# The PLE gate of a hybrid MLA/GLA layer on one core: its first 512 columns as one block of 512 in place of two of 256

## The chip, the cores and the metric

The kernel runs on one core of a Trainium2 chip. The metric is device microseconds of one execution; the figure of a kernel is the median of its runs. A trace of one profiled execution stands beside it: for each engine (PE for the matrix engine, DVE for vectors, ACT for activations, POOL, and SP, which issues the DMAs) when each instruction ran and what it waited for.

## What is computed

One layer, 1024 tokens, model width 1024, all in fp32: an input projection, latent attention (MLA, 8 heads, 64 columns without and 32 with rotary position) and a gated linear attention (GLA) side by side, a sigmoid-gated merge, an output projection, and at the end a gate of per-layer embeddings:

```
merged = sigmoid(merge_a) * y_a + sigmoid(merge_b) * y_b
x = x + merged @ w_out[l]

e = rmsnorm(p[l] @ w_ple[l], ple_norm_g[l])
g_ple = jax.nn.sigmoid(rmsnorm(x, ple_gate_norm_g[l]) @ w_ple_gate[l])
x = x + g_ple * e
return rmsnorm(x, final_norm_g)
```

The change is in the second last product, `rmsnorm(x) @ w_ple_gate`, which is 1024 x 1024 by 1024 x 1024.

## The kernel before

**Precision and matmuls.** Each fp32 operand is kept as a high part (fp32r) and a low rest. `split` makes them: ACT copies the high part (L127), DVE subtracts (L128). A product is three matmuls (`mm3`, L145 to L147): high by high, high by low, low by high. A weight tile is loaded by SP (`load_w`, L137) and split.

**Buffers.** Nearly everything takes its memory from numbered slots of 128 x 1024 fp32 (512 KB): `alloc` takes the slot that has been free the longest, `drop` gives it back. There are NSLOT = 35, and NMORE = 4 more are opened when the GLA part is over.

**Order of work.** The program is written as generators that are advanced in turn, but the order on each engine is not the written one: a scheduler places all instructions by a timeline of its own when the program is built, for all engines at once, and waits between engines are set after that. So each engine and SP run a fixed list.

**Attention** (about 500 to 760 us). Heads go in pairs. `make_pair` projects q and then k of both heads in one product, in two halves of 512 tokens, and splits the result into the odd head's buffers (qh, ql, kh, kl). The even head's 64 rows are then copied to its own buffers by DMA (L864: qh<-qh, ql<-ql, kh<-kh, kl<-kl), and after such a copy has landed the odd head's rotary rows are written over the place they came from (L871 for q, L867 for k). `scores` and `weighted` follow for each head and each half: scores s (L145 to L147), row maximum (L914), exp (L924), transposes of p into pt (L963) and their split, products o with vp (L954, L955), and og (L976 to L978) with a gate gt that was loaded (L945) and scaled with the row sums that came through DRAM (L943, L946). Units of work of several heads and of other parts (the q/k projection of the next pair from w_qk and w_qr, and `embed`, which computes e from in_pT and in_w_ple and scales it by in_ple_g, gb) lie between them. The y projection (from oh, ol, the split of og) begins before the last head is done and adds to ta (L992, L993), which is split into mh, ml.

**Gate** (881 us on). `stream` multiplies by w_out, and x2 and its normed, transposed parts gh, gl come out (L1126, L1127). `load_pg` loads gate weights: w_pgA for the first 512 columns, in two halves of 256 with two tiles each (each tile holds 4 of the 8 row blocks), w_pgB for the last 512 with four tiles. For each of the two halves and each of the 8 token blocks `block` makes 24 matmuls of 256 columns, a tanh (L1183), two DVE products (L1184, L1186) and a square with a row sum (L1188). Then come the last 512 columns, where each token block's row sum is finished, its scale is found (`newton1`) and it is written out (L1216 to L1221); the last token block is cut in two of 256 columns.

Of the kernel before, what the change touches and what calls it, by code (L numbers as in the profile page):

```python
# [16 lines left out]
P = 128  # L17
S = 1024
D = 1024
HALF = 512  # L20
# [1 line left out]
HEADS = 8  # L22
SCALE = (64 + 32) ** -0.5
NSLOT = 35
NMORE = 4
NTMP = 6
NG = 6

# [24 lines left out]
def hybrid_kernel(tc, a, out):  # L53
    nc = tc.nc
    from contextlib import ExitStack

    with ExitStack() as ctx:
# [12 lines left out]
        def uid(name):  # L70
            count[0] += 1
            return f"{name}_{count[0]}"
# [7 lines left out]
        def drop(*ts):  # L80
            for t in ts:
                if id(t) in held:
                    i, _ = held.pop(id(t))
                    free.append(i)
# [4 lines left out]
        def t2(name, dt=F32):  # L89
            return tp.tile([P, HALF], dt, tag="t2", name=uid(name))  # L90
# [44 lines left out]
        def load_w(src, w, eng=None):  # L135
            raw = alloc(F32, "wr")
            nc.sync.dma_start(raw[:, :w], src)  # L137
            hi = alloc(F32R, "wh")
            lo = hi[:, HALF:S] if w <= HALF else alloc(F32R, "wl")
            split(hi[:, :w], lo[:, :w], raw[:, :w], eng)  # L140
            drop(raw)
            return hi, lo
# [103 lines left out]
        d_e = [dr.tile([P, S], F32, name=f"d_e{m}") for m in range(8)]  # L246
# [25 lines left out]
        with tc.tile_pool(name="ps0", bufs=1, space=PSUM) as ps0:  # L272
# [162 lines left out]
            for tb in range(8):  # L435
                ps = get("d", "gv")
                for kt in range(8):
                    hi, lo = wv[kt // 2]
                    c = slice((kt % 2) * HALF, (kt % 2 + 1) * HALF)
# [11 lines left out]
        with tc.tile_pool(name="psG", bufs=1, space=PSUM) as psG:  # L451
# [293 lines left out]
            pools[1] = ctx.enter_context(tc.tile_pool(name="slots2", bufs=1))  # L745
            free.extend(range(NSLOT, NSLOT + NMORE))

# [52 lines left out]
        with tc.tile_pool(name="psB", bufs=1, space=PSUM) as psB:  # L800
# [75 lines left out]
            for tb in range(8):  # L876
                ps = get("d", "v")
                hi, lo = wv_
                for kt in range(2):
                    c = slice(kt * HALF, (kt + 1) * HALF)  # L880
# [176 lines left out]
            for n in range(16):  # L1057
# [6 lines left out]
                per = 2 if hf == 0 else 1  # L1064
# [42 lines left out]
        with tc.tile_pool(name="psC", bufs=1, space=PSUM) as psC:  # L1107
            get = psum_pool({"d": (HALF, 5), "t": (HALF, 3)}, psC)
            getC.append(get)
            for n, _ in enumerate(ya):  # L1110
                if n == 11 - n_pre:
                    w_first = load_w(a["w_out"][0:P, :], S)
            drop(*ooh, *ool)


            gh, gl = [], []
            x2 = big(F32, "x2")
            x2m = x2.rearrange("p (t c) -> p t c", t=8)

            def ev_x2(m):  # L1120
                def ev(h, ps):
                    if h == 0:
                        gh.append(alloc(F32R, "gh"))
                        gl.append(alloc(F32R, "gl"))
                    xs = t2("xr")
                    nc.sync.dma_start(xs, a["xT"][m * P : (m + 1) * P, hs(h)])  # L1126
                    nc.vector.scalar_tensor_tensor(xs, ps, 0.5, xs, op0=ALU.mult, op1=ALU.add)  # L1127
                    split_gain(gh[m][:, hs(h)], gl[m][:, hs(h)], xs, col(V_PG + m))
                    late.append((m, h, xs))

                return ev

            def turn():
                m, h, xs = late.pop(0)
                pt = get("t", "xt")
                for j in range(4):
                    nc.tensor.transpose(pt[:, j * P : (j + 1) * P], xs[:, j * P : (j + 1) * P], ident)
                nc.scalar.activation(x2m[:, 4 * h : 4 * h + 4, m * P : (m + 1) * P], pt.rearrange("p (t c) -> p t c", t=4), AF.Copy)

            late = []  # L1140

            def load_pg(b):
                src, n = (a["w_pgA"][b * P : (b + 1) * P], 2) if b < 2 else (a["w_pgB"], 4)
                return [load_w(src[:, j * S : (j + 1) * S], S) for j in range(n)]

            wpg = [None] * 3
            jobs = [(a["w_out"][m * P : (m + 1) * P, :], P, 8, ev_x2(m)) for m in range(8)]
            for n, _ in enumerate(stream(get, jobs, mh, ml, w_first)):
                if n == 15:
                    wpg[0] = load_pg(0)  # L1150
                if n > 1:
                    turn()
            turn()
            drop(*mh, *ml)

            fg = alloc(F32, "fg")
            nc.sync.dma_start(fg, a["fin_g"].to_broadcast([P, S]))
            r2 = []
            dn = cp.tile([P, 1], F32, name="dn")
            nc.gpsimd.memset(dn, D * EPS)  # L1160
            for tb in range(8):
                s1, r = small("x2s", 1), small("x2r", 1, bufs=8)
                sq = alloc(F32, "sq")
                nc.scalar.activation(sq, x2m[:, tb, :], AF.Square, accum_out=s1)
                drop(sq)
                newton1(r, s1, dn, D)
                nc.vector.tensor_scalar(r, r, 0.5, None, op0=ALU.mult)
                r2.append(r)
            s3 = cp.tile([P, 32], F32, name="s3")
            QW = 256  # L1170

            def block(tb, b, c0, w, et):

                bw, per = (QW, 4) if b < 2 else (HALF, 2)
                o = b * QW + c0
                ps = get("d", "pg")
                for kt in range(8):
                    hi, lo = wpg[b][kt // per]
                    c = slice((kt % per) * bw + c0, (kt % per) * bw + c0 + w)
                    xs = slice(tb * P, (tb + 1) * P)  # L1180
                    mm3(ps[:, :w], gh[kt][:, xs], gl[kt][:, xs], hi[:, c], lo[:, c], kt == 0, kt == 7)
                g_ = t2("g")[:, :w]
                nc.scalar.activation(g_, ps[:, :w], AF.Tanh, scale=r2[tb])  # L1183
                nc.vector.scalar_tensor_tensor(et, g_, 1.0, et, op0=ALU.add, op1=ALU.mult)  # L1184
                xq = x2m[:, tb, o : o + w]
                nc.vector.scalar_tensor_tensor(xq, et, re_[:, tb : tb + 1], xq, op0=ALU.mult, op1=ALU.add)  # L1186
                k = tb * 4 + b + (c0 > 0)
                nc.scalar.activation(g_, xq, AF.Square, accum_out=s3[:, k : k + 1])  # L1188

            for b in range(2):  # L1190
                wpg[b + 1] = load_pg(b + 1)
                for tb in range(8):
                    et = t2("et")[:, :QW]
                    nc.sync.dma_start(et, d_e[tb][:, b * QW : (b + 1) * QW])
                    block(tb, b, 0, QW, et)
                for w_ in wpg[b]:
                    drop(*w_)
            ets = []
            for tb in range(8):
                ets.append(alloc(F32, "et"))  # L1200
                nc.sync.dma_start(ets[tb][:, :HALF], d_e[tb][:, HALF:S])
            for tb in range(8):

                cut = HALF if tb < 7 else 256
                k0, n = tb * 4, 2 + (tb == 7)
                if tb == 7:
                    block(tb, 2, 0, cut, ets[tb][:, 0:cut])
                s1, r = small("fs", 1), small("fr", 1)
                nc.vector.tensor_reduce(s1, s3[:, k0 : k0 + n], axis=mybir.AxisListType.X, op=ALU.add)
                nc.vector.tensor_scalar(s1, s1, D * EPS, None, op0=ALU.add)  # L1210
                c0 = cut % HALF
                block(tb, 2, c0, HALF - c0, ets[tb][:, c0:HALF])
                newton1(r, s3[:, k0 + n : k0 + n + 1], s1, D)
                for h in range(2):
                    xo = x2m[:, tb, hs(h)]
                    nc.gpsimd.tensor_tensor(xo, xo, fg[:, hs(h)], op=ALU.mult)  # L1216
                    if h:
                        nc.scalar.activation(xo, xo, AF.Copy, scale=r)
                    else:
                        nc.vector.tensor_scalar(xo, xo, r, None, op0=ALU.mult)  # L1220
                    nc.sync.dma_start(out[tb * P : (tb + 1) * P, hs(h)], xo)  # L1221
# [3 lines left out]
def _tiles(w, cols, width=P):  # L1225

    K = w.shape[0]
    n = len(cols) // width
    w = w[:, np.asarray(cols)].reshape(K // P, P, n, width)
    return np.ascontiguousarray(w.transpose(2, 1, 0, 3).reshape(n * P, K // P * width))  # L1230
# [26 lines left out]
def _layout(inputs):  # L1257
    g = {k: np.asarray(v) for k, v in inputs.items()}
    o = {}
# [3 lines left out]
    w = g["w_in"][0]  # L1263
# [9 lines left out]
    for pr in range(4):  # L1273
        A, B = 2 * pr, 2 * pr + 1
        n = np.concatenate([np.arange(h * 96, h * 96 + 64) for h in (A, B)])
# [7 lines left out]
    full = np.arange(D)  # L1283
# [1 line left out]
    o["w_gla_br"] = _tiles(g["w_gla_br"][0], full)  # L1285
    o["w_out"] = _tiles(g["w_out"][0], full)
    o["w_ple"] = np.ascontiguousarray(g["w_ple"][0])
    o["w_pgA"] = _tiles(g["w_ple_gate"][0], full[:512], 256)
    o["w_pgB"] = _tiles(g["w_ple_gate"][0], full[512:], 512)
    o["ple_g"] = np.ascontiguousarray(g["ple_norm_g"]).reshape(1, D)  # L1290
    o["fin_g"] = np.ascontiguousarray(g["final_norm_g"]).reshape(1, D)
    o["w_gk_up"] = np.ascontiguousarray(np.tile(g["w_gk_up"][0], (4, 1)))
# [22 lines left out]
```

## Time and profile before

| | us |
|---|---|
| median of 3 runs (lowest, highest) | 984.31 (984.19, 984.76) |
| the profiled execution | 983.49 |
| its span in the trace | 981.7 |
| PE busy in it | 955.8 |
| granted clock of PE, mean | 0.99 |
| first matmul of the gate at | 881.2 |

The span runs from the first instruction to the last; 1.8 us of the execution lie around it. The profiled execution is 0.8 us under the median. A row of a list of instructions gives start, duration, engine, line, operation, output <- inputs, and in square brackets the idle time in front with the one that ended it. Matmuls overlap in the records, so their pace is read from start to start.

### The profile page before, as it was taken

The page shows a single profiled execution, that of the slowest core. Times are in us where ns is not written, and L with a number is a line of the kernel's source. Part 1 is how long each engine was busy: PE and PEld are TensorE (multiplying, and loading weights), DVE is VectorE, ACT ScalarE, POOL GpSimd, SP SyncE. Part 2 cuts the span into 40 slices and gives each one's busy share as a digit, 9 for nine tenths or more (in the row PEclk, how much of TensorE's full clock was granted, in tenths as well). Part 3 has the DMA queues.
Part 4 walks back from the last instruction along what each step waited for, and adds up shares of the span by engine and source line. Part 5 has one row for each costly group of instructions (what it writes and reads, how often), then busy time and mean ns, then how long its engine had stood idle before and what let it go on. Part 6 is the DMA issues. An engine that isn't in the chain of part 4 may idle for free.

```text
span 981.7 us, 14101 instructions
## 1 busy us (share of the span) xinstructions
PE 955.8 (97%) x5216; PEld 794.3 (81%) x5216; DVE 590.2 (60%) x1227; ACT 413.1 (42%) x800; POOL 128.1 (13%) x103
## 2 busy tenths in 40 slices
PE   7999999999999999999999999997999999999995
PEld 5887877887887887888888778886888788889985
DVE  6737765574474474433476469785757863239666
ACT  7306731331331342321333257676885432228333
POOL 2100000000000000001101012235363000000422
PEclk9999999999999999999999999997999999999998
DMA  7200211122222122211253844537146761136112
GB/s 281 94 22 22 65 43 43 57 84 86 76 108 86 63 79 86 97 65 43 82 181 127 230 121 121 133 98 177 49 147 229 254 208 65 49 119 188 53 69 103
DMA packets 47828, 105.70 MB, mean 108 GB/s; under 512 B 6736, under 2 KB 9616, under 8 KB 47760
## 3 DMA queue, kind: packets, MB, share of 16 engines
q1 hardware_dynamic: 47760, 104.81, 33.1%
q8 instruction: 41, 0.67, 0.3%
q14 instruction: 27, 0.22, 0.1%
HBM read 72.18 MB, written 25.20 MB: 99 GB/s over the span
## 4 chain that ended last, share of the span: by engine, by line
PE 86%; DVE 6%; ACT 3%; DMA 3%; issue 2%; SPq 0%; DVEq 0%; ACTq 0%
PE d L145 19%; PE d L147 18%; PE d L146 18%; PE pt L963 3%; PE pg L147 3%; PE pg L146 3%; PE pg L145 3%; PE L L559 2%; PE o L955 2%; PE s L146 2%; PE o L954 2%; PE s L147 2%; PE s L145 2%; PE o L690 1%; DMA kl<-kl 1%
## 5 line engine op out<-in xcount | busy, mean ns | idle before, releaser
L145 PE MATMUL d<-xh,wh 128*128 128x512 f32 x544 | 215.9, 400 | 2.8 <-ACT xh L132 2.6
L146 PE MATMUL d<-xl,wh 128*128 128x512 f32 x544 | 214.5, 395 | 0.1
L147 PE MATMUL d<-xh,wl 128*128 128x512 f32 x544 | 213.3, 393 | 0.1
L145 PEld LDWEIGHTS d<-xh,wh 128*128 128x128 f32 x544 | 103.0, 190 | 28.1 <-ACT xh L132 4.6
L127 ACT ACTIVATE wh<-wr 128x1024 fp32r<-128x1024 f32 (+4 forms) x81 | 76.2, 943 | 114.3 <-DMA wr<-in_w_in 40.4
L146 PEld LDWEIGHTS d<-xl,wh 128*128 128x128 f32 x544 | 103.0, 189 | 21.9 <-DVE xl L133 0.8
L147 PEld LDWEIGHTS d<-xh,wl 128*128 128x128 f32 x544 | 102.7, 189 | 21.9 <-DVE wl L128 0.5
L128 DVE TENSOR_TENSOR wl<-wr,wh 128x1024 fp32r<-128x1024 f32 (+2 forms) x59 | 74.6, 1267 | 71.2 <-ACT wh L127 71.1
L145 PE MATMUL pg<-wh,gh 128*128 128x256 f32 (+1 forms) x200 | 62.7, 314 | 0.0
L146 PE MATMUL pg<-wl,gh 128*128 128x256 f32 (+1 forms) x200 | 62.5, 313 | 0.0
L147 PE MATMUL pg<-wh,gl 128*128 128x256 f32 (+1 forms) x200 | 62.5, 313 | 0.0
L128 DVE TENSOR_TENSOR pt<-pt,pt 128x512 fp32r<-128x512 f32 (+1 forms) x96 | 51.4, 550 | 17.1 <-ACT pt L127 16.9
L494 ACT ACTIVATE z<-z 128x512 f32<-128x512 f32 x32 | 20.2, 631 | 98.0 <-DVE z L466 94.2
L924 ACT ACTIVATE p<-p,nm 128x128 f32<-128x128 f32 (+3 forms) x64 | 49.3, 772 | 21.2 <-DVE nm L914 21.1
L466 DVE TENSOR_TENSOR z<-d,rb 128x512 f32<-128x512 f32 x32 | 22.1, 690 | 51.3 <-PE d L147 51.3
L127 ACT ACTIVATE pt<-pt 128x512 fp32r<-128x512 f32 (+1 forms) x96 | 44.6, 485 | 15.5 <-PE pt L963 13.6
L145 PE MATMUL d<-mh,wh 128*128 128x512 f32 x128 | 50.7, 399 | 0.0
L146 PE MATMUL d<-ol,wh 128*128 128x512 f32 x128 | 50.1, 392 | 0.4 <-DVE ol L128 0.4
L147 PE MATMUL d<-mh,wl 128*128 128x512 f32 x128 | 50.2, 392 | 0.0
L147 PE MATMUL d<-oh,wh 128*128 128x512 f32 x128 | 50.1, 391 | 0.0
L146 PE MATMUL d<-ml,wh 128*128 128x512 f32 x128 | 49.9, 390 | 0.0
L145 PE MATMUL d<-oh,wh 128*128 128x512 f32 x128 | 49.9, 395 | 0.0
(263 smaller groups left out, 1924.4 us busy)
## 6 DMA issues: line engine op xcount, KB each, us to landing
wr<-in_w_in SPq DMA_DIRECT2D x33, 512.0 KB
d_ta<-z SPq DMA_DIRECT2D x16, 256.0 KB
d_tb<-z SPq DMA_DIRECT2D x16, 256.0 KB
tb<-d_tb SPq DMA_DIRECT2D x16, 256.0 KB
d_zb<-tb SPq DMA_DIRECT2D x16, 256.0 KB
d_e<-er SPq DMA_DIRECT2D x16, 256.0 KB
ta<-d_ta SPq DMA_DIRECT2D x16, 256.0 KB
zb<-d_zb SPq DMA_DIRECT2D x16, 256.0 KB
```

The source lines that it names most:

```text
L127: nc.scalar.activation(dst_hi, src, AF.Copy)
L128: (eng or nc.vector).tensor_tensor(dst_lo, src, f(dst_hi), op=ALU.subtract)
L145: nc.tensor.matmul(ps, lh, rh, start=first, stop=False)
L146: nc.tensor.matmul(ps, lh, rl, start=False, stop=False)
L147: nc.tensor.matmul(ps, ll, rh, start=False, stop=last)
L466: nc.vector.tensor_tensor(z, ps, rb[:, hs(h)], op=ALU.mult)
L494: nc.scalar.activation(z, z, AF.Tanh, scale=0.5)
L559: nc.tensor.matmul(L[:, hd * HALF + c * P : hd * HALF + (c + 1) * P], lt[rows(hd), cs], rt[rows(hd), cs], start=True, stop=True,)
L924: nc.scalar.activation(pt[:, :w], pt[:, :w], AF.Exp, bias=nm, scale=-1.0, accum_out=den)
L954: nc.tensor.matmul(po[:, n0:], vv, ts_[:, n0:HALF], start=kb == 0, stop=False)
L955: nc.tensor.matmul(po[:, n0:], vv, ts_[:, HALF + n0 : S], start=False, stop=kb == nk - 1)
L963: nc.tensor.transpose(pt[:, j * P : (j + 1) * P], pq[j][:, kb * P : (kb + 1) * P], ident)
```

## The change

NMORE becomes 8, and the scratch that the program sets aside for DMAs with dynamic addresses becomes 1024 bytes, which makes room for the four slots. The gate's weight becomes one array w_pg of two halves of 512 columns, four tiles each; the first half is one pass over the token blocks with blocks of 512, as the second was. The row sums have one column fewer per token block.

```diff
-NMORE = 4
+NMORE = 8
...
             def load_pg(b):
-                src, n = (a["w_pgA"][b * P : (b + 1) * P], 2) if b < 2 else (a["w_pgB"], 4)
-                return [load_w(src[:, j * S : (j + 1) * S], S) for j in range(n)]
-
-            wpg = [None] * 3
+                return [load_w(a["w_pg"][b * P : (b + 1) * P, j * S : (j + 1) * S], S) for j in range(4)]
+
+            wpg = [None] * 2
...
-                bw, per = (QW, 4) if b < 2 else (HALF, 2)
-                o = b * QW + c0
+                o = b * HALF + c0
                 ps = get("d", "pg")
                 for kt in range(8):
-                    hi, lo = wpg[b][kt // per]
-                    c = slice((kt % per) * bw + c0, (kt % per) * bw + c0 + w)
+                    hi, lo = wpg[b][kt // 2]
+                    c = slice((kt % 2) * HALF + c0, (kt % 2) * HALF + c0 + w)
...
-            for b in range(2):
-                wpg[b + 1] = load_pg(b + 1)
-                for tb in range(8):
-                    et = t2("et")[:, :QW]
-                    nc.sync.dma_start(et, d_e[tb][:, b * QW : (b + 1) * QW])
-                    block(tb, b, 0, QW, et)
-                for w_ in wpg[b]:
-                    drop(*w_)
+            wpg[1] = load_pg(1)
+            for tb in range(8):
+                et = t2("et")
+                nc.sync.dma_start(et, d_e[tb][:, 0:HALF])
+                block(tb, 0, 0, HALF, et)
+            for w_ in wpg[0]:
+                drop(*w_)
...
-                k0, n = tb * 4, 2 + (tb == 7)
+                k0, n = tb * 4, 1 + (tb == 7)
...
-    nc = bacc.Bacc("TRN2", target_bir_lowering=False, num_devices=1)
+    nc = bacc.Bacc("TRN2", target_bir_lowering=False, num_devices=1, dynamic_dma_scratch_size=1024)
```

PE has 192 matmuls fewer (5216 before, 5024 now). Up to the beginning of the attention the order on PE is the same; from the first head on the scheduler has placed the instructions anew. In the gate, the first four loads of w_pg stand among the loads of xr (L1126) of the w_out stream, where before the first load of w_pgA stood behind them. Three places of the attention follow, before and now.

**SP, the load of w_qk for the q/k projection of pair 1 (heads 2 and 3).** wr_685 is the load; kh_706 to kl_709 and qh_702 to ql_705 belong to that pair, tb and d_zb to the merge's data on their way through DRAM. Before:

```order
L780 DMA d_zb7_134<-tb_668_4429 128x512
L845 DMA kl_708_4550<-krt_93_620 32x1024
L849 DMA qh_702_4544<-d_rq00_123 16x1024 x2
L137 DMA wr_685_4499<-in_w_qk 128x640
L780 DMA d_zb7_134<-tb_676_4467 128x512
L943 DMA d_rc1_108<-rr_694_4517 4x128
L849 DMA ql_704_4546<-d_rq01_124 16x1024 x2
L946 DMA rB_696_4521<-d_rc1_108 64x512
```

Now:

```order
L946 DMA rB_655_4364<-d_rc0_107 64x512
L778 DMA tb_660_4390<-d_tb6_105 128x512
L137 DMA wr_685_4499<-in_w_qk 128x640
L778 DMA tb_668_4429<-d_tb7_106 128x512
L137 DMA wr_713_4577<-in_w_qr 128x384
L778 DMA tb_676_4467<-d_tb7_106 128x512
L945 DMA gt_695_4520<-d_gm0_87 64x512
```

The load stands between two loads of tb and ahead of w_qr; before it was behind w_qr and the q rows.

**PE, the first scores of head 6 (pair 3).** s_1090 is the first; kh_1022 and kl_1024 are head 6's copies, o_1062 an earlier unit's product. Before:

```order
L954 MATMUL o_1062_5839<-pt_1064_5845,vp_3967 128x512
L955 MATMUL o_1062_5839<-pt_1064_5845,vp_3967 128x512
L954 MATMUL o_1062_5839<-pt_1070_5871,vp_3967 128x384
L145 MATMUL s_1090_5933<-kh_1022_5667,qh_1018_5663 128x128
L146 MATMUL s_1090_5933<-kl_1024_5669,qh_1018_5663 128x128
L147 MATMUL s_1090_5933<-kh_1022_5667,ql_1020_5665 128x128
L955 MATMUL o_1062_5839<-pt_1070_5871,vp_3967 128x384
L954 MATMUL o_1062_5839<-pt_1076_5892,vp_3967 128x256
L145 MATMUL s_1104_5975<-kh_1022_5667,qh_1018_5663 128x256
```

Now:

```order
L954 MATMUL o_1062_5839<-pt_1064_5845,vp_3967 128x512
L955 MATMUL o_1062_5839<-pt_1064_5845,vp_3967 128x512
L145 MATMUL s_1090_5933<-kh_1022_5667,qh_1018_5663 128x128
L145 MATMUL s_1104_5975<-kh_1022_5667,qh_1018_5663 128x256
L145 MATMUL s_1113_6008<-kh_1022_5667,qh_1018_5663 128x384
L939 MATMUL rcT_1092_5940<-ident_69,rc_1081_5910 4x128
L954 MATMUL o_1062_5839<-pt_1070_5871,vp_3967 128x384
L955 MATMUL o_1062_5839<-pt_1070_5871,vp_3967 128x384
L954 MATMUL o_1062_5839<-pt_1076_5892,vp_3967 128x256
L963 MATMUL pt_1097_5951<-ident_69,p_1049_5811 128x128
L963 MATMUL pt_1097_5951<-ident_69,p_1050_5812 128x128
```

The three kh products of three score tiles stand first, and their kl products (L146) follow behind sixteen transposes, two of which are shown. Ahead of s_1090 the score tiles s_1071, s_1073 and s_1077 of another head stood between the k projection and it; they are in front of the projection's end now.

**SP, the copies of pair 3.** qh_1018, ql_1020, kh_1022 and kl_1024 are head 6, the numbers one higher head 7. Before:

```order
L137 DMA wr_1110_6002<-in_pT 128x1024
L137 DMA wr_1119_6034<-in_w_ple 128x1024
L864 DMA qh_1018_5663<-qh_1019_5664 64x1024
L864 DMA ql_1020_5665<-ql_1021_5666 64x1024
L871 DMA qh_1019_5664<-d_rq10_125 16x1024 x4
L871 DMA ql_1021_5666<-d_rq11_126 16x1024 x2
L137 DMA wr_1084_5924<-in_pT 128x1024
L871 DMA ql_1021_5666<-d_rq11_126 16x1024
L864 DMA kh_1022_5667<-kh_1023_5668 64x1024
L943 DMA d_rc10_117<-rr_1059_5831 4x128
L864 DMA kl_1024_5669<-kl_1025_5670 64x1024
L137 DMA wr_1101_5969<-in_w_ple 128x1024
```

Now:

```order
L137 DMA wr_1119_6034<-in_w_ple 128x1024
L137 DMA wr_1084_5924<-in_pT 128x1024
L864 DMA qh_1018_5663<-qh_1019_5664 64x1024
L864 DMA ql_1020_5665<-ql_1021_5666 64x1024
L871 DMA qh_1019_5664<-d_rq10_125 16x1024 x4
L871 DMA ql_1021_5666<-d_rq11_126 16x1024 x4
L137 DMA wr_1110_6002<-in_pT 128x1024
L864 DMA kh_1022_5667<-kh_1023_5668 64x1024
L1023 DMA gb_1129_6064<-in_ple_g 128x1024
L864 DMA kl_1024_5669<-kl_1025_5670 64x1024
```

All four ql rows stand ahead of the second load of in_pT and of kh's copy, and the load of in_ple_g (gb) is between kh's copy and kl's. Before, one of the ql rows stood behind kl's copy, and gb ten rows further down.

**DVE, where the last head's og joins the y projection.** og_1181 is the last head's output, ol_1284 its low part, wl_1386 a weight tile of w_out, ta and ml the y projection's results. Before:

```order
L992 SCALAR_TENSOR_TENSOR ta_1350_6862<-ta_1350_6862,d_1347_6847 128x512
L977 TENSOR_TENSOR og_1181_6241<-o_1293_6632,og_1181_6241 64x512
L993 TENSOR_TENSOR ta_1350_6862<-ta_1350_6862,zb_1351_6863 128x512
L128 TENSOR_TENSOR wl_1386_7061<-wr_1384_7058,wh_1385_7060 128x1024
L128 TENSOR_TENSOR ml_1349_6861<-ta_1350_6862,mh_1348_6860 128x512
L128 TENSOR_TENSOR ol_1284_6609<-og_1181_6241,oh_1283_6608 128x512
L992 SCALAR_TENSOR_TENSOR ta_1353_6889<-ta_1353_6889,d_1352_6876 128x512
```

Now:

```order
L992 SCALAR_TENSOR_TENSOR ta_1350_6862<-ta_1350_6862,d_1347_6847 128x512
L128 TENSOR_TENSOR ml_1342_6828<-ta_1343_6829,mh_1341_6827 128x512
L977 TENSOR_TENSOR og_1181_6241<-o_1293_6632,og_1181_6241 64x512
L993 TENSOR_TENSOR ta_1350_6862<-ta_1350_6862,zb_1351_6863 128x512
L128 TENSOR_TENSOR ml_1349_6861<-ta_1350_6862,mh_1348_6860 128x512
L128 TENSOR_TENSOR ol_1284_6609<-og_1181_6241,oh_1283_6608 128x512
L992 SCALAR_TENSOR_TENSOR ta_1353_6889<-ta_1353_6889,d_1352_6876 128x512
```

The weight split wl_1386 no longer stands between og and ol.

## Rows read from the trace of the kernel before

**Rows 1.** The profile's page: busy time of each engine; the chain's shares by engine.
```profile
PE 955.8 (97%) x5216; PEld 794.3 (81%) x5216; DVE 590.2 (60%) x1227; ACT 413.1 (42%) x800; POOL 128.1 (13%) x103
...
PE 86%; DVE 6%; ACT 3%; DMA 3%; issue 2%; SPq 0%; DVEq 0%; ACTq 0%
```
**Rows 2.** By stretch: length, PE, PEld, DVE, ACT, POOL, granted clock, DMA share, GB/s.
```profile
500.00:600.00 100.00, 97.34 (x484) 80.75 (x483) 67.23 (x152) 41.57 (x91) 11.52 (x9) 1.00 0.55 161
600.00:700.00 100.00, 92.64 (x524) 80.14 (x524) 75.04 (x207) 69.00 (x153) 33.06 (x22) 0.93 0.43 115
```
**Rows 3.** PE's waits from 400 us on: in total, times, longest.
```profile
PE s L145 <- DVE pt L128: 5.5, 1, 5.5
```
**Rows 4.** PE in the gate: a block's first matmul, at three places.
```profile
887.50 0.28 PE L145 MATMUL pg<-wh,gh 128*128 128x256 f32 x1
...
927.82 0.40 PE L145 MATMUL pg<-wh,gh 128*128 128x512 f32 x1
...
965.92 0.28 PE L145 MATMUL pg<-wh,gh 128*128 128x256 f32 x1
```
**Rows 5.** By stretch, as rows 2, beside small and beside large blocks.
```profile
895.00:900.00 5.00, 5.00 (x44) 5.00 (x44) 4.87 (x29) 4.39 (x11) 0.00 (x0) 1.00 0.59 187
...
940.00:945.00 5.00, 5.00 (x24) 4.14 (x23) 3.62 (x14) 1.58 (x5) 1.29 (x1) 1.00 0.28 105
```
**Rows 6.** SP, chain and PE around the w_qk load of pair 1.
```profile
558.67 1.67 SPq L778 DMA_DIRECT2D tb<-d_tb  x3
...
568.61 4.04 DMA wr<-in_w_qk
...
573.47 0.50 PE L145 MATMUL d<-ch,wh 128*128 128x512 f32 x1 [0.76 <-ACT wh L127]
573.80 0.40 PE L146 MATMUL d<-cl,wh 128*128 128x512 f32 x1
574.33 0.50 PE L147 MATMUL d<-ch,wl 128*128 128x512 f32 x1
```
**Rows 7.** SP and PE: the copies of head 2 and its first scores.
```profile
589.11 0.47 SPq L864 DMA_DIRECT2D kh<-kh  x1
...
590.37 0.59 SPq L864 DMA_DIRECT2D kl<-kl  x1
...
594.05 0.33 PE L146 MATMUL s<-kl,qh 96*128 96x128 f32 x1 [0.78 <-DMA ql<-d_rq]
```
**Rows 8.** Chain and PE: kl's copy of head 4 and its first use.
```profile
630.75 3.66 DMA kl<-kl
...
634.46 0.33 PE L146 MATMUL s<-kl,qh 96*128 96x128 f32 x1 [0.83 <-DMA kl<-kl]
```
**Rows 9.** SP, chain and PE: the copies of head 6 and its first scores.
```profile
668.38 1.72 SPq L871 DMA_DIRECT2D qh<-d_rq  x4
...
671.07 0.42 SPq L137 DMA_DIRECT2D wr<-in_pT  x1
...
672.06 0.47 SPq L864 DMA_DIRECT2D kh<-kh  x1
...
673.15 5.92 DMA kl<-kl
...
678.01 0.44 PE L145 MATMUL s<-kh,qh 96*128 96x128 f32 x1 [5.53 <-DVE pt L128]
```
**Rows 10.** By stretch, as rows 2, around head 6's first scores.
```profile
675.00:680.00 5.00, 1.33 (x4) 1.17 (x5) 1.29 (x4) 2.52 (x5) 2.35 (x1) 0.50 1.00 229
680.00:685.00 5.00, 5.00 (x17) 4.46 (x17) 2.87 (x10) 4.11 (x9) 3.33 (x2) 0.50 0.54 126
685.00:690.00 5.00, 5.00 (x29) 4.78 (x28) 3.36 (x9) 3.65 (x10) 1.60 (x2) 0.69 0.32 132
```
**Rows 11.** PE and DVE where attention joins the y projection.
```profile
759.57 0.22 PE L955 MATMUL o<-pt,vp 128*128 128x128 f32 x1
...
762.47 2.32 DVE L128 TENSOR_TENSOR wl<-wr,wh 128x1024 fp32r<-128x1024 f32 x1
...
765.31 0.68 DVE L128 TENSOR_TENSOR ol<-og,oh 128x512 fp32r<-128x512 f32 x1
...
766.04 0.50 PE L146 MATMUL d<-ol,wh 128*128 128x512 f32 x1 [0.42 <-DVE ol L128]
```

More of the change, by code (lines that the diff above doesn't have):

```diff
@@ L1169, in hybrid_kernel @@
             s3 = cp.tile([P, 32], F32, name="s3")
-            QW = 256
             def block(tb, b, c0, w, et):
-                bw, per = (QW, 4) if b < 2 else (HALF, 2)
-                o = b * QW + c0
+                o = b * HALF + c0
                 ps = get("d", "pg")
                 for kt in range(8):
-                    hi, lo = wpg[b][kt // per]
-                    c = slice((kt % per) * bw + c0, (kt % per) * bw + c0 + w)
+                    hi, lo = wpg[b][kt // 2]
+                    c = slice((kt % 2) * HALF + c0, (kt % 2) * HALF + c0 + w)
                     xs = slice(tb * P, (tb + 1) * P)
@@ L1204, in hybrid_kernel @@
                 cut = HALF if tb < 7 else 256
-                k0, n = tb * 4, 2 + (tb == 7)
+                k0, n = tb * 4, 1 + (tb == 7)
                 if tb == 7:
-                    block(tb, 2, 0, cut, ets[tb][:, 0:cut])
+                    block(tb, 1, 0, cut, ets[tb][:, 0:cut])
                 s1, r = small("fs", 1), small("fr", 1)
@@ L1211, in hybrid_kernel @@
                 c0 = cut % HALF
-                block(tb, 2, c0, HALF - c0, ets[tb][:, c0:HALF])
+                block(tb, 1, c0, HALF - c0, ets[tb][:, c0:HALF])
                 newton1(r, s3[:, k0 + n : k0 + n + 1], s1, D)
@@ L1287, in _layout @@
     o["w_ple"] = np.ascontiguousarray(g["w_ple"][0])
-    o["w_pgA"] = _tiles(g["w_ple_gate"][0], full[:512], 256)
-    o["w_pgB"] = _tiles(g["w_ple_gate"][0], full[512:], 512)
+    o["w_pg"] = _tiles(g["w_ple_gate"][0], full, 512)
     o["ple_g"] = np.ascontiguousarray(g["ple_norm_g"]).reshape(1, D)
```

## The prediction

> **What bounds the kernel now.** I read the engines' busy times and the chain of work first: TensorE (PE) is busy for 955.8 of 981.7 us and carries 86% of the chain [rows 1]. A table of the span in pieces of 100 us then says where it is not: between 500 and 600 it misses 2.7 us, between 600 and 700 it misses 7.4 at a mean granted clock of 0.93 [rows 2]. So time can be won in two ways: fewer or faster matmuls where PE is full, or waits that go away between 500 and 770. In the list of PE's waits from 400 on one entry is 5.5 us long, before a score matmul [rows 3]; the others are under 1 us each. The edit is made in the gate, where PE is full; but a program sets the order of the work, and it has set the attention's order anew too. The sum therefore has one part for the gate and one for each place of the attention that moved.
>
> **Part 1, the gate.** Before, sixteen blocks of 256 columns are followed by seven and a half of 512 and two last ones of 256. Fourteen of the small blocks run from 887.50 to 927.82, 40.32 us or 2.88 each, and seven large ones from there to 965.92, 38.10 us or 5.44 each [rows 4]. Each has 24 matmuls: 120.0 ns for 256 columns, 226.8 ns for 512. Two small blocks cost 5.76, one large one 5.44. PE is busy for 5.00 of 5 us in both stretches, so these are paces and not waits; the weight loads fill 5.00 of 5 us beside the small blocks and 4.14 beside the large ones [rows 5], which fits a small matmul that can't be over before the next weights are in. Eight pairs become eight single blocks: 8 x (5.76 - 5.44) = **-2.5 us**. That a large block in the first half runs as the large ones do now is the only assumption; the bounds are 0 (no gain in pace) and -2.5.
>
> The Trainium skill, "TensorE: Matmul & The Clock Gate", section "Back-to-back issue gap", gives the columns at 2.4 GHz plus 2.5 ns for a matmul by itself. By it two of 256 against one of 512 differ by 2.5 ns only, 192 times over 0.5 us in all, and the sum below would end 2.0 us higher. The rows of this loop contradict it (120.0 against 226.8 ns), so the measurement decides, and it has no chance of its own.
>
> On the other engines there is less work: beside the small blocks ACT is busy 4.39 of 5 us and DVE 4.87, beside the large ones 1.58 and 3.62 [rows 5]. PE waits for neither, at 5.00 of 5; so what is taken away there is hidden and costs or brings nothing. The end of the kernel is the same instructions.
>
> **Part 2, attention.** Four more slots and the new gate make the scheduler place PE, SP's DMAs and the splits differently from the first head on. I went through the places where PE waits now.
>
> *Pair 1, weights.* w_qk is issued at 568.61 and takes 4.04 us, then ACT and DVE split it. The projection waits 0.76 us before its first matmul and some 0.3 before its third, which starts 0.53 after the second where 0.23 is the pace [rows 6]; with the pieces between, 1.3 us more than the columns need. In the changed order the load stands some ten rows earlier on SP, between two of the tb loads that went out from 558.67 on [rows 6]. **-1.3 us** (bounds -1.3 and 0).
>
> *Pair 1, copies.* An even head's k (kh, kl) is projected in the odd head's buffer and copied by DMA; the first scores wait for it. Now kh goes out at 589.11, kl at 590.37, and PE waits 0.78 before kl's first use at 594.05 [rows 7] (the row names the ql load, which ends at the same moment; the matmul reads kl and qh, both copies). With the piece before it that is 0.95. Counting the order at 227 ns for each matmul of 512 columns, 5.5 us of other PE work stand between the end of the k projection and the first scores; afterwards 2.4. And SP has all four ql rows ahead of kh, not one, at some 0.43 each (four take 1.72 in [rows 9]): kh about 1.3 us later. The projection itself stands about 3 us later, so that the split ends no sooner than SP is free. kh goes out at 590.6 and lands, if a copy takes 2.9 to 3.7 (kl's 3.66 at head 4 is one with no other large load [rows 8]), at 593.5 to 594.3, where PE is there at 591.9: a wait of 1.6 to 2.4, then up to 1.0 for kl, less the 0.95 of now. **+2.2 us** (bounds +0.7, only kh's shorter wait, and +3.1, the whole work that has gone from between).
>
> *Pair 2, copies.* 4.2 us of other work become 2.4, but kl's first use moves back by 2.8. PE waits 0.83 for kl now [rows 8]: **+0.4** (bounds -0.8, that wait hidden, and +1.0).
>
> *Pair 3 (head 6).* This is the large wait. The row names DVE as what ended it, but the matmul that stands there at 678.01 needs the copy kh<-kh, issued at 672.06; kl<-kl, from 673.15, took 5.92 us [rows 9], with a 512-KB load issued at 671.07 beside it and the DMA engines at 1.00 [rows 10]. The copies go out late since SP stands at qh's copy until 668.38 [rows 9], behind two other loads of 512 KB. PE idles 5.5 us, the granted clock falls to 0.50 (1.2 GHz), still 0.69 as a mean of 685 to 690 [rows 10]; some 10 us run at half, about 5 us lost. With about 1 us that PE then waits for kl the place costs near 12. In the new order the same loads stand in front of qh's copy, a pT load still in front of kh, and the 512-KB load gb goes out between kh and kl: nothing sends the copies earlier. The other work ahead of the first use shrinks from 5.2 to 2.8 us, of which 1.3 is a projection that comes later: the wait grows by 1.1 to 2.4. Sixteen transposes (with products near 3.1 us) now stand between the first kh and kl uses, so the second wait of about 1.0 goes, unless gb delays kl. **+1.0** (bounds -3, a copy as short as head 4's, and +3). The clock falls as before.
>
> *Join of attention and the y projection.* After the last o product (759.57) og, oh and ol go through ACT, DVE, POOL, ACT and DVE, and PE waits 0.42 for ol at 766.04 [rows 11]. ol starts at 765.31, since a split of 2.32 us from 762.47 stands in front [rows 11]. That split moves ahead, which lets ol start about 0.9 earlier; but PE has 2.8 us of other work until oh's first use, and 3.6 until ol's, in place of 4.9 and 5.7. oh is ready about 4.6 us after the product: a wait of 1.8 against some 0.6 now. **+1.2** (bounds +0.5, +2.0).
>
> **Sum.** -2.5 - 1.3 + 2.2 + 0.4 + 1.0 + 1.2 = **+1.0 us**. The profiled execution took 983.49 us (span 981.7), so the same execution with the edit would take 984.5. The median of the runs is 984.31, 0.8 higher; I put the sum on it: **985.3**. About 0.2% or 2.0 us (982.3 to 986.3) is what a measurement of this kernel can tell from no change. With each term at its lower bound the sum is -6.4, at its upper +9.1: 977.9 to 993.4.
>
> **Rivals.**
> *Only the gains count.* The scheduler put the first scores nearer to the projection because it has other work to give PE elsewhere; if the copies come as fast as the shortest here and the join is covered, -2.5 and -1.3 remain with perhaps +1: 980.5 to 982. For it: both gains are read directly. Against it: three even heads lose cover at once. Chance 0.21.
> *Head 6 comes in time.* If qh's copy starts ahead of the two 512-KB loads, kh lands near 672, the waits of 5.5 and 1.0 us go and the clock stays at 1.00: up to -11.8, 973 to 979. Against it: SP's order keeps these loads in front. Chance 0.10.
> *A second fall of the clock (slower).* The place is the first scores of head 2. If kh lands 3 us or more after PE is there, PE stands nearly as long as in the one wait that lowered the clock, 5.5 us [rows 3], and longer than in the waits of 0.8 that did not [rows 7, 8]. The price is that of head 6, up to 5 us on top of the wait: 987 to 992. In this case I count the same copies without the clock, all at their upper bounds, too. For it: the new order sends four small rows ahead of kh, and at head 6 a 512-KB load between. Chance 0.30.
> *The change doesn't do what it says.* A large block needs four weight tiles in its pass, a small one two; if they came late, PE would wait in the gate for a load and a split, 2 to 4 us: 987 to 989. Against it: the four loads stand among the loads of xr in the w_out stream, ahead of where the first two stood. Chance 0.02.
>
> **Numbers.** Forecast (982.3 to 986.3) 0.37; faster 0.21 + 0.10 = 0.31; slower 0.30 + 0.02 = 0.32. The range leaves out most of the head-6 case (under 979) and the worst of the clock case (over 990.5), some 0.15 in all: 979.0 to 990.5.
>
> **What the profile after would show.** Gate: 24 matmuls at 227 ns from about 881 on, weight loads at 4.1 of 5 us throughout; else part 1 is wrong. List of waits: the w_qk entry gone; waits at the first scores of heads 2, 4 and 6, the last still over 5 us with a clock of 0.50 behind it. A clock of 1.00 in the whole stretch from 600 to 700, or a second fall near 595, would make the prediction wrong; so would waits of PE inside the gate.

## The result, and the profile after

The changed kernel takes 992.87 us (median of 4 runs, 992.63 to 994.54) beside 984.25 for the kernel before on the same chip (4 runs, 982.82 to 984.76): a ratio of 1.0094 with a 95% interval of 1.0076 to 1.0111. It is **slower by 8.6 us**, where 985.3 was forecast with a range of 979.0 to 990.5. The profiled execution took 992.73 us, its span is 991.0, 9.3 longer than before.

The page of the kernel after, its busy times, answers to [rows 1]:

```profile
PE 958.3 (97%) x5024; PEld 785.6 (79%) x5024; DVE 584.4 (59%) x1211; ACT 411.0 (41%) x776; POOL 128.3 (13%) x103
```

192 matmuls fewer, and PE is busy for longer. By stretches of 100 us (length, PE, PEld, DVE, ACT, POOL, granted clock, DMA share, GB/s), the answer to [rows 2]; the last line, in a fence of its own, is the kernel before from 700 to 800:

```profile
500.00:600.00 100.00, 95.23 (x454) 79.09 (x453) 63.01 (x141) 39.46 (x84) 9.69 (x7) 0.98 0.53 157
600.00:700.00 100.00, 93.40 (x528) 79.45 (x528) 74.76 (x200) 68.95 (x154) 35.13 (x24) 0.95 0.43 119
700.00:800.00 100.00, 95.12 (x468) 78.02 (x468) 71.72 (x148) 61.83 (x131) 33.65 (x25) 1.00 0.57 183
```
```profile
700.00:800.00 100.00, 99.58 (x488) 82.51 (x487) 74.52 (x141) 61.70 (x130) 33.50 (x25) 1.00 0.62 205
```

Between 600 and 700 PE is now busy for longer than before (93.40 for 92.64), between 500 and 600 less (95.23 for 97.34), and between 700 and 800, where before it was full to 0.4 us, it misses 4.9. The list of PE's waits from 400 on (in total, times, longest) has grown from seven entries to eleven; the largest:

```profile
PE s L145 <- DMA kh<-kh: 5.5, 3, 3.5
PE o L955 <- DVE pt L128: 2.9, 4, 1.4
PE s L145 <- issue: 2.4, 1, 2.4
PE d L145 <- ACT oh L127: 1.8, 1, 1.8
PE rcT L939 <- DVE pt L128: 1.1, 1, 1.1
PE o L954 <- ACT pt L127: 0.7, 2, 0.5
```

The one wait of 5.5 us [rows 3], at head 6, is now 3.5 us long, and a wait of 1.75 for the copy of head 2 and a short one stand beside it under the same name. The 2.4 us called "issue" (the profile names nothing that ended them) are head 0's first scores, where 0.95 stood before. And a kind that the kernel before had nowhere is there: o products that wait for the split of pt. Head 0's row, before and after:

```profile
549.12 0.65 PE L145 MATMUL s<-kh,qh 96*128 96x128 f32 x3 [0.95 <-issue]
```
```profile
551.39 1.08 PE L145 MATMUL s<-kh,qh 96*128 96x128 f32 x3 [2.41 <-issue]
```

**The gate did what was forecast.** Two rows of the trace frame the last part of the kernel: the transposes xt of x (first and last start), and the gate's last matmuls. Before, then after:

```profile
L1137 PE MATMUL xt<-ident,xr x64: 270/272/273, 803.3 to 885.2; 128*128 128x128 f32 x64
...
L147 PE MATMUL pg<-wh,gl x200: 278/283/389, 881.6 to 971.6; 128*128 128x256 f32 x72, 128*128 128x512 f32 x28
```
```profile
L1137 PE MATMUL xt<-ident,xr x64: 270/272/273, 815.4 to 898.5; 128*128 128x128 f32 x64
...
L147 PE MATMUL pg<-wh,gl x136: 279/389/398, 893.1 to 980.4; 128*128 128x512 f32 x120, 128*128 128x256 f32 x16
```

From the first transpose to the last gate matmul it is 168.3 us before and 165.0 after; 0.7 of the 3.3 are three matmuls of another product that stand ahead of the first transpose now, the rest is the gate's 2.5. The first transpose is 12.1 us later, though. All of the loss lies ahead of it.

**Where it was lost.** From PE's timeline I took, for each pair of neighbouring matmuls, the time between their starts less what such a pair usually takes in the kernel before (227 ns after 512 columns, 120 after 256, 110 between transposes), and added up by place. A matmul at half the clock counts in this as lost time, too.

| place (times of the kernel after) | before, us | after, us | difference | forecast |
|---|---|---|---|---|
| first stage, at 46 | 0 | 0.9 | +0.9 | none |
| head 0, first scores, 550 to 555 | 1.5 | 4.6 | **+3.1** | none |
| w_qk of pair 1 | 1.9 | 0.3 | -1.6 | -1.3 |
| head 2, first scores, 595 to 605 | 2.1 | 5.5 | +3.4 | +2.2 |
| head 4 and around, 610 to 660 | 4.7 | 6.2 | +1.5 | +0.4 |
| head 6, 660 to 710 | 13.4 | 11.8 | -1.6 | +1.0 |
| o products, 710 to 760 | 2.3 | 6.5 | **+4.2** | none |
| join, 776 | 0.8 | 2.3 | +1.5 | +1.2 |
| gate | | | -2.5 | -2.5 |
| behind the last matmul | 10.1 | 10.5 | +0.4 | none |

The differences add to 9.3 us, the growth of the span. The six places that the prediction priced add to +0.7, and it had said +1.0. The other four, which it didn't price, add to 8.6.

**The clock.** Mean granted clock by 5 us in the kernel after:

```profile
550.00:555.00 5.00, 3.61 (x10) 3.08 (x11) 0.00 (x0) 0.00 (x0) 0.00 (x0) 0.66 0.74 208
...
595.00:600.00 5.00, 2.70 (x14) 2.17 (x13) 3.15 (x11) 3.67 (x11) 1.27 (x1) 0.91 0.77 167
600.00:605.00 5.00, 5.00 (x28) 4.41 (x28) 2.44 (x9) 2.66 (x8) 1.27 (x1) 0.75 0.36 96
680.00:685.00 5.00, 1.54 (x8) 0.63 (x6) 3.10 (x8) 4.24 (x8) 1.26 (x1) 0.94 0.86 237
685.00:690.00 5.00, 4.45 (x20) 4.31 (x21) 0.97 (x2) 0.83 (x3) 2.36 (x1) 0.50 0.86 225
690.00:695.00 5.00, 5.00 (x31) 4.58 (x30) 3.93 (x11) 4.95 (x11) 1.59 (x2) 0.87 0.57 171
```

One fall has become three. At 1.2 instead of 2.4 GHz a row's mean of 0.66 is 3.4 of its 5 us; the same sum over 595 to 605 gives 3.4, over 680 to 695 some 7. Together that is the 13.7 us of before [rows 10], where 3.6 of them fell into PE's idle time. So the falls cost about 1 us more than before in all, some 1.6 each at head 0 and head 2 and half of what it was at head 6.

**The waits behind 730.** ACT and PE in the kernel after (start, length, engine, line, operation, and the idle time before it with what ended it):

```profile
756.18 0.63 ACT L127 ACTIVATE wh<-wr 128x512 fp32r<-128x512 f32 x1 [1.68 <-DMA wr<-in_w_mla_br]
756.72 1.07 ACT L127 ACTIVATE pt<-pt 128x512 fp32r<-128x512 f32 x2
```
```profile
756.69 0.50 PE L955 MATMUL o<-pt,vp 128*128 128x512 f32 x1 [1.39 <-DVE pt L128]
...
758.67 0.50 PE L955 MATMUL o<-pt,vp 128*128 128x512 f32 x1 [0.82 <-DVE pt L128]
...
776.24 1.19 PE L145 MATMUL d<-oh,wh 128*128 128x512 f32 x4 [1.76 <-ACT oh L127]
```

ACT stands for 1.68 us at the split of a weight tile whose load hasn't landed, and the split of pt is queued behind it. SP stood at stores of e tiles, which POOL had not finished, before it issued that load. The waits of SP from 715 to 765, before and after:

```profile
SPq L1035 <- POOL er L1034: 12.5, 10, 2.6
```
```profile
SPq L1035 <- POOL er L1034: 18.8, 10, 6.2
```

ACT's own wait for these loads is hardly longer than it was, though: 7.3 us from 715 to 765 before, 7.5 after. In the kernel before, too, a split of pt followed such a wait (at 752.56, behind 3.65 us of it), but its first product stood on PE at 755.08, behind other work. So a late load alone doesn't make PE wait; what is new is how soon PE comes to the product. ACT before:

```profile
ACT wh L127 <- DMA wr<-in_w_mla_br: 7.3, 5, 3.7
```

### The profile page after: what moved, and what is told of

Its sections match the earlier page's. It is cut to its first block, busy times and chain, and to the rows that moved or that the text cites. A ratio compares the mean times of both kernels' runs of the same rounds, so it can differ in the third digit from the quotient of the medians.

```text
span 991.0 us, 13641 instructions
## 1 busy us (share of the span) xinstructions
PE 958.3 (97%) x5024; PEld 785.6 (79%) x5024; DVE 584.4 (59%) x1211; ACT 411.0 (41%) x776; POOL 128.3 (13%) x103
## 5 line engine op out<-in xcount | busy, mean ns | idle before, releaser
L146 PE MATMUL d<-xl,wh 128*128 128x512 f32 x544 | 214.5, 395 | 0.1
L146 PEld LDWEIGHTS d<-xl,wh 128*128 128x128 f32 x544 | 103.0, 189 | 22.0 <-DVE xl L133 0.8
L128 DVE TENSOR_TENSOR wl<-wr,wh 128x1024 fp32r<-128x1024 f32 (+2 forms) x59 | 72.5, 1231 | 57.9 <-ACT wh L127 54.4
L145 PE MATMUL pg<-wh,gh 128*128 128x512 f32 (+1 forms) x136 | 51.4, 378 | 0.0
L147 PE MATMUL pg<-wh,gl 128*128 128x512 f32 (+1 forms) x136 | 51.2, 377 | 0.0
L146 PE MATMUL pg<-wl,gh 128*128 128x512 f32 (+1 forms) x136 | 51.2, 377 | 0.0
L146 PE MATMUL d<-ol,wh 128*128 128x512 f32 x128 | 50.4, 394 | 0.0
L146 PE MATMUL d<-ml,wh 128*128 128x512 f32 x128 | 50.1, 391 | 0.0
```

The source lines that it names most:

```text
L128: (eng or nc.vector).tensor_tensor(dst_lo, src, f(dst_hi), op=ALU.subtract)
L145: nc.tensor.matmul(ps, lh, rh, start=first, stop=False)
L146: nc.tensor.matmul(ps, lh, rl, start=False, stop=False)
L147: nc.tensor.matmul(ps, ll, rh, start=False, stop=last)
```

## The experiments

All ratios are to the kernel before, run in turn with it on the same chip. The kernel before scattered more in these runs than above (980.8 to 989.5 in the 20 of the first round), so ratios are compared, not times.

**Is it the slots or the blocks?** Two kernels take the change apart. The first is the kernel before with the slots alone:

```diff
-NMORE = 4
+NMORE = 8
...
-    nc = bacc.Bacc("TRN2", target_bir_lowering=False, num_devices=1)
+    nc = bacc.Bacc("TRN2", target_bir_lowering=False, num_devices=1, dynamic_dma_scratch_size=1024)
```

> The kernel before, its gate in blocks of 256 untouched, with the eight slots (and the small DMA scratch) alone. On PE its fixed order is that of the changed kernel, instruction by instruction, until well behind the attention. Theory A (the loss is the attention's new order, which the four slots bring; the gate's blocks have no part in it): 995.4 us, 2.5 more than the changed kernel's 992.9, with the granted clock falling near 551, 599 and 684 as there. Theory B (the large blocks bring the loss, by their loads or by what they do to the order): 984 to 985, as before.

Measured: 1.0080 (1.0052 to 1.0107), median 994.84. In its trace the first xt starts at the same time as in the changed kernel, and only the gate is longer:

```profile
L1137 PE MATMUL xt<-ident,xr x64: 270/272/273, 815.4 to 895.8; 128*128 128x128 f32 x64
...
L147 PE MATMUL pg<-wh,gl x200: 279/283/389, 892.9 to 982.9; 128*128 128x256 f32 x72, 128*128 128x512 f32 x28
```

The gate with small blocks ends at 982.9, with large ones at 980.4: 2.5 us. That the first xt comes at the same time is partly chance. The clock doesn't fall near 551 as theory A had it, and head 0 loses 1.9 us for 4.6; instead it falls near 757, and PE loses 2.0 us more than the changed kernel between 739 and 764. The ratio, too, doesn't show the 2.5 us (1.0080 here, 1.0094 for the changed kernel); they are read from the traces. The second is the changed kernel, whose last four slots are handed out when the attention is over:

```diff
-            free.extend(range(NSLOT, NSLOT + NMORE))
+            free.extend(range(NSLOT, NSLOT + 4))
...
+            free.extend(range(NSLOT + 4, NSLOT + NMORE))
+
             def load_pg(b):
```

> The changed kernel with eight slots, but the last four are handed out only when the gate's first weights are loaded. On PE its order is that of the kernel before until the attention is over. Theory A (the slots' order): 981.7 us, the 984.25 of before less 2.5 in the gate, one fall of the clock near 674. Theory B (the large blocks): 990 to 993. Theory C (the smaller DMA scratch slows every transfer): 988 or more.

Measured: 0.9971 (0.9948 to 0.9994), 2.9 us faster than before. Its large waits are those of the kernel before (the row of 5.4 is head 6, now under the name of the copy), and so is its one fall of the clock, of 13.7 us:

```profile
PE s L145 <- DMA kl<-kl: 5.4, 1, 5.4
PE s L146 <- DMA kl<-kl: 1.3, 2, 0.8
PE s L145 <- issue: 1.0, 1, 1.0
PE s L146 <- DMA ql<-d_rq: 0.8, 1, 0.8
```

Theory A holds in what it says of the cause; B and C (the scratch) fall. The blocks bring 2.5 us. What the four slots cost, by the order that they bring to the attention, is 8 us by the ratio of the first kernel, 12 by the distance between the changed kernel and the second, and 11.3 by the spans of the traces (993.1 for 981.7).

**Is it the number of slots?** The kernel before with five and with seven more slots (NMORE = 5, NMORE = 7, and the scratch):

> The kernel before with five more slots in place of four (and the small DMA scratch), gate untouched. Theory A' (any other number of slots gives another order, and the time follows from where the copies of the even heads fall in it, not from the number): somewhere from 980 to 998, with waits at first scores of heads 0, 2, 4 or 6 making the difference. Rival (more slots let more be loaded ahead, and this crowds the transfers): about 987, a quarter of the way to eight.

> As the last with seven more slots. Theory A': somewhere from 980 to 998, in no order with four, five and eight. Rival (crowding): about 992, three quarters of the way to the 995 of eight.

Measured: 1.0086 (1.0061 to 1.0112) with five, 1.0078 (1.0052 to 1.0104) with seven. With eight it was 1.0080. It doesn't grow with the number, so crowding is out, and one slot more than four costs as much as four more. That they agree so well I had not expected; it may say that four is a good order rather than that eight is a bad one, but fewer than four were not run. The waits with seven:

```profile
PE s L145 <- DMA kh<-kh: 5.6, 3, 3.0
PE s L145 <- DVE pt L128: 3.5, 3, 1.9
PE o L955 <- DVE pt L128: 2.9, 4, 2.2
PE o L954 <- ACT pt L127: 1.5, 3, 0.9
```

The same two kinds as in the changed kernel: several shorter waits for kh in place of one long one, and o products that wait for the split of pt. From 750 to 760 the kernels with five, seven and eight slots lose 4.8, 4.8 and 4.1 us by the account above, the changed kernel 3.2, the kernel before 0.3.

**The waits for pt.** The changed kernel, its stores of e issued by POOL:

```diff
-                        nc.sync.dma_start(d_e[tb][:, hs(c)], er)
+                        nc.gpsimd.dma_start(d_e[tb][:, hs(c)], er)
```

> The changed kernel, with the stores of the scaled e tiles issued by POOL, which makes them, instead of SP, which waited 18.8 us in all for them between 715 and 765. PE's order is that of the changed kernel until behind head 6's first scores. Theory D (the waits for pt splits at 730 and 756 to 759, 4.2 us, come from SP standing at a store, a w_mla_br load issued late behind it, and ACT standing at that load with a pt split behind): 988 to 990 beside 992.9, these waits gone, those of heads 0, 2 and 6 unchanged. Rival (they come from the place of the splits on DVE and ACT alone): 992 to 994.

Measured: 1.0051 (1.0033 to 1.0068), median 989.70; by the ratios 0.4% or some 4 us less than the changed kernel. ACT's wait for these loads from 715 to 765, in the changed kernel and here:

```profile
ACT wh L127 <- DMA wr<-in_w_mla_br: 7.5, 4, 2.9
```
```profile
ACT wh L127 <- DMA wr<-in_w_mla_br: 3.8, 5, 1.4
```

PE's waits for pt between 750 and 760 are gone, by the same account as above 0.3 us for 3.2; around 730 nearly the same is lost as before (1.5 for 1.6). The join became longer in turn (3.4 for 2.1), and a product of e waits 1.7 for POOL, which now also issues stores: together they take back what the waits gave. The span is still 1.6 us shorter than the changed kernel's (989.4 for 991.0); what is gained lies from 660 to 710, where the clock is down for 3.4 us in place of 6.8 and PE waits less for pt splits before head 6. And PE's order is the changed kernel's only until 721, so the places where theory D was to be tested stand in another order. It fits the waits that went; it is not shown by the time. The same edit to the kernel with the late slots, which has no such waits:

> The same edit to the kernel with the late slots. It has no such waits after 700 but 0.4 at the join; so by theory D nothing is to be had: within 1.5 us of the kernel with the late slots (0.997 of before). If SP's place behind the stores costs more than the waits show, 2 us or more faster.

Measured: 1.0025 (1.0003 to 1.0047), where 0.9971 plus or minus 0.0015 was expected. A miss: it costs half a per cent. The profiled execution is its slowest (993.65, median 987.0). In it PE has the same order as the kernel before until 734, and yet is 8.5 us later there: at head 0 it waits 2.65 us where it waited 1.0, and at 550 to 565 it runs at half the clock. So one order on PE costs more in one execution than in another; why this kernel costs more so often stays open.

What head 0 costs can be followed through the traces. PE's first score and SP's first row of L867, which both need kh's copy, start there within 0.1 us of each other in each. From the issue of that copy to the score, and what PE loses from 540 to 566 by the account above (the table there takes other bounds):

| kernel | PE's order ahead of head 0 | copy to score, us | lost, us |
|---|---|---|---|
| before | old | 6.3 | 1.3 |
| late slots | old | 6.1 | 1.4 |
| late slots, loads on POOL (below) | old | 7.0 | 3.7 |
| late slots, stores on POOL | old | 7.8 | 9.0 |
| slots alone | new | 6.7 | 1.9 |
| changed | new | 7.9 | 4.6 |
| changed, stores on POOL | new | 8.5 | 5.3 |

The new order has one wide matmul less ahead of the score (0.23 us). The loss goes with how long the copy takes in one execution, and both orders have had short and long ones. So the +3.1 of the table above is not shown to belong to the new order.

**Do the copies' landings set the waits at the first scores?** Each copy is cut in two of 512 tokens, and the first is sent when the first half is projected:

```diff
                     for h in range(2):
                         bank(get, hi, lo, P, c0, range(n), xh_, xl_, h, ev(x))
+                        for nm in (x + "h", x + "l"):
+                            t0, t1 = f(qk[nm, 2 * pr]), f(qk[nm, 2 * pr + 1])
+                            nc.sync.dma_start(t0[0:64, hs(h)], t1[0:64, hs(h)])
                         yield
                     for y in range(2):
                         nm = x + "hl"[y]
-                        t0, t1 = f(qk[nm, 2 * pr]), f(qk[nm, 2 * pr + 1])
-                        nc.sync.dma_start(t0[0:64], t1[0:64])
+                        t1 = f(qk[nm, 2 * pr + 1])
```

> The changed kernel, with each copy of an even head's q and k rows cut in two of 512 tokens, the first sent as soon as the first half is projected. The first scores read the first 128 tokens only. Theory E (the waits at heads 0, 2 and 6 end when the copies land): these waits, 9 us with their falls of the clock, shrink by half or more, 985 to 990. Rival (the transfers are full there, and the smaller copies land no sooner): 991 to 995.

> The same edit to the kernel with the late slots. Theory E: the waits at heads 0, 2 and 4 (4 us) and the one at head 6 (5.5 us and a fall of the clock of 13.7 us) shrink: 972 to 979. Rival: 981 to 986.

Measured: 1.0102 (1.0071 to 1.0134) in the changed kernel, 0.9901 (0.9877 to 0.9925) with the late slots. The first looks like the rival, but its waits say otherwise. From 400 to 660, and behind 660:

```profile
PE o L956 <- ACT pt L127: 1.7, 1, 1.7
PE o L956 <- DVE og L979: 1.1, 2, 0.9
...
PE s L145 <- DVE tb L779: 0.3, 1, 0.3
```
```profile
PE o L957 <- DVE pt L128: 5.4, 3, 3.0
PE e L146 <- POOL wl L128: 3.6, 1, 3.6
PE o L956 <- ACT pt L127: 2.8, 2, 2.1
PE s L146 <- DMA kl<-kl: 2.1, 1, 2.1
```

The score waits of heads 0 and 2 are gone (their places lose 0.6 and 1.4 us by the account above, for 4.6 and 5.5), and that of head 6 is down to 2.1. But the edit made yet another order from head 0 on, in which the stretch from 660 to 770 loses some 9 us more than in the changed kernel, on o and e products above all. So the waits fit theory E, though with the order changed as well the copies alone are not shown to be the reason, and the time of the kernel followed something else. With the late slots the new order is a good one; the waits from 400 on:

```profile
PE rcT L941 <- DVE rc L929: 4.6, 1, 4.6
PE o L956 <- ACT pt L127: 1.4, 1, 1.4
PE s L146 <- DMA kl<-kl: 1.3, 2, 1.1
PE s L145 <- DMA kh<-kh: 1.1, 1, 1.1
```

976.86 us beside 986.84 for the kernel before: **this version beats both**, by 1.0% and some 1.9%. Between 500 and 600 PE is full to 0.35 us.

**What makes head 6's copies late?** Two attempts, both on the kernel with the late slots: all copies of q and k rows issued by POOL, and the 512-KB loads of in_pT and in_w_ple issued by POOL.

```diff
-                        nc.sync.dma_start(t0[0:64], t1[0:64])
+                        nc.gpsimd.dma_start(t0[0:64], t1[0:64])
```

> As e2_late, and the copies of an even head's q and k rows (four for each pair) are issued by POOL instead of SP, whose queue they then don't stand in. If the wait at head 6 is SP's queue (copies issued 3 us after the split of k is done, behind qh's copy and six small loads), the wait of 5.5 us and the fall of the clock go: 971 to 977. If it is the transfer itself, among loads of 512 KB, or if POOL issues more slowly: 979 to 984, with the wait still over 3 us.

```diff
-        nc.sync.dma_start(raw[:, :w], src)
+        (eng or nc.sync).dma_start(raw[:, :w], src)
```

> The kernel with the late slots, its four 512-KB loads of in_pT and in_w_ple issued by POOL, so that on SP nothing stands between the copies of pair 3 but small rows; the order on DVE is the same, on PE until head 6. If the wait at head 6 comes from SP standing at those loads: 973 to 979, the wait under 2 us. If it comes from the transfers running beside the copies, or from the copies' place behind qh's: 980 to 985.

Measured: 1.0001 (0.9976 to 1.0025) and 0.9987 (0.9966 to 1.0009). Neither is a gain. With the loads on POOL the copies of head 6 on SP (start, length of the issue) and PE's wait are:

```profile
662.59 0.49 SPq L864 DMA_DIRECT2D qh<-qh  x1
...
670.20 1.70 SPq L871 DMA_DIRECT2D qh<-d_rq  x4
...
673.54 0.47 SPq L864 DMA_DIRECT2D kh<-kh  x1
```

From the issue of qh's copy to the row that has to wait for its landing it is 7.6 us, where it was 7.3 in the kernel before and 7.7 with the late slots alone, though none of these loads stands on SP any more; the DMA engines are at 0.99 from 664 to 666. The wait at head 6 is 5.6 us. So it isn't that SP stands at the loads. What is left is that they move beside the copies, or that kh's copy stands on SP behind qh's landing; the two are not told apart. With the copies on POOL the wait for kh goes, and a wait of 6.0 us of an o product for a split of pt comes to the same place, since ACT stands there at a tile of in_pT, which SP issued at 675.70 and which took 6.99 us to land. PE's order is another from head 0 on in that kernel, too. Taking the loads themselves away from there wasn't tried.

## Why the prediction was wrong

*Part 1, the gate: right.* -2.5 us forecast, and 2.5 in both pairs of traces with one order (980.4 and 982.9; before and the late slots, 168.3 and 165.3 from the first transpose to the end, of which 0.5 are two matmuls of another product that stand ahead of it now). Large blocks in the first half run as those in the second: from 926 to 936 the weight loads take 8.28 of 10 us, as [rows 5] has them beside large blocks (4.14 of 5).

```profile
926.00:936.00 10.00, 10.00 (x45) 8.28 (x45) 3.18 (x4) 2.83 (x6) 3.78 (x3) 1.00 0.09 26
```

*Part 2, the steps taken: nearly right in sum, not one by one.* w_qk -1.6 (-1.3 forecast), head 2 +3.4 (+2.2; the waits of 1.75 and 0.55 us are as forecast, and a fall of the clock adds some 1.6), head 4 +1.5 (+0.4; 1.1 of it is a small transpose that waits for DVE, not the copies), head 6 -1.6 (+1.0), join +1.5 (+1.2). With the gate +0.7 for +1.0: that the sum came so near is luck, since misses of +1.2, +1.1 and -2.6 cancel in it. At head 6 the mis-sized term is the work at half the clock: the wait itself is 3.5 us for 5.5 and not 6.6 to 7.9, and the clock is down for 7 us instead of 13.7. PE came later to it, having waited 2.2 us in small pieces, most of it for pt splits, since 677.

*The step that failed is a sentence*: "I went through the places where PE waits now." A place that was not on that list stands in the sum at nothing, without a reason, and these places brought +8.6 of the 9.3 us. A new order has its waits where the old one had none: the o products, with no wait in the old trace, now wait for splits of pt (+4.2 us). These stand on ACT and DVE behind splits of w_mla_br tiles, and from 750 to 760 PE loses 3.2 to 4.8 us in the traces with five, seven and eight slots. Head 0's first scores (+3.1) stood in the old list with a wait of 1 us that the prediction didn't price; that one could not be read from the order, since it goes, in seven traces, with the landing of one copy. The split wl_1386, which the prediction saw "moves ahead" and booked as a gain, is not what PE waits for: the splits of w_out tiles of 1024 columns start on DVE at 764.49 and 766.82, behind the waits for pt. Loads that land late were there before as well; at this place the new order has PE come to the product sooner. Why the scheduler places it so stays open.

*The rivals.* The one on the slower side named head 2 and a second fall of the clock near 595: both are there, and the second fall is one of the signs that the prediction had named for being wrong; but the fall costs some 1.6 us and not 5. It was priced by head 6's, where the clock was down for 13.7 us; the time would have been reached only with head 0 and the o products added. "Only the gains count" is what the kernel with the late slots does: it lies at 0.9971, near the 980.5 to 982 said for it. "Head 6 comes in time" didn't happen in any kernel.

*The range* was made of bounds of the listed terms, up to +9.1 (993.4), and then cut at 990.5. The uncut one would have held the measured 992.87, but by luck: the listed terms add to +0.7. It had no term for places not looked at. The first stage's +0.9 is none of the change's: PE has one order there, and the kernels here are between 0.2 us earlier and 1.4 later than before at 494 us, ahead of the attention.

## What to carry to other kernels

When a scheduler orders the whole program, an edit that changes the buffers' number or turn is a change everywhere from where they are first handed out: read the new order of every queue there, and ask for each row that moved forward what now stands behind it, not only what happens to the old waits. If only one stage needs the buffers, hand them out at that stage; here that kept the old order and turned +0.9% into -0.3%. And an edit to a kernel with a tuned order is best judged twice, in the old order and in the new one, before its own worth is spoken of.

## What was not expected of the hardware

A wait of PE of 2.4 us at head 0 was followed by a fall of the clock to 1.2 GHz, while one of 1.2 us at the same place in the kernel with the slots alone was not. The length of the wait alone doesn't say how long the clock stays down: 3.4 us after that one, 13.7 us after the 5.5 us of the kernel before, and 13.7 us, too, after 2.65 us at head 0 in the kernel with the late slots and the stores on POOL. And a copy of 256 KB from SBUF to SBUF took from 3.66 us [rows 8] to 8.5 us from its issue to the first score that needs it, at head 0. What moved beside it is likely to set this, but it was not taken apart. PE came 8.5 us later to 734 in one execution than in another with the same order of its matmuls.
